# A gated-unit kernel: a small copy as the first DMA on the scalar queue, 512 bytes in each of sixteen rows

## Chip, cores and metric

One core of a Trainium2 chip. The metric is the device time of one execution in microseconds (us).

## The reference

```python
def setup_inputs():
    return {"x": np.random.randn(8192, 8192).astype(np.float32)}

def reference(x):
    a, b = np.split(x, 2, axis=-1)
    return a * (1 / (1 + np.exp(-b)))
```

268 MB are read, 134 MB written, and each output element costs one sigmoid and one multiply.

## The kernel before

The input is cut into 32 tiles of 256 rows. A tile puts two whole rows on each of 128 partitions, so one partition's part is a contiguous 64 KB of input and 32 KB of output. There are two input slots and two output slots in SBUF, the memory on the chip that the compute engines work from; DRAM holds input and output. Loads are issued on the sync queue, stores on the scalar queue. The first and the last tile are computed in four parts, the last is also stored in four parts.

```python
    R = 2
    SLOTS = 2
    n_tiles = n_rows // (P * R)
    x_t = x.rearrange("(n p r) m -> n p (r m)", p=P, r=R)
    out_t = out.rearrange("(n p r) m -> n p (r m)", p=P, r=R)
    ...
    for i in range(n_tiles):
        ...
        load = nc.sync.dma_start(out=xs[i % SLOTS], in_=x_t[i])
        ...
        def store(cols):
            ins = nc.scalar.dma_start(out=out_t[i, :, cols], in_=os[i % SLOTS][:, cols])
            now["stores"].append(ins)

        for k, (r, c) in enumerate(parts):
            b = rows[:, r, 1, c]
            sig = nc.scalar.activation(out=b, in_=b, func=SIG)
            mul = nc.vector.tensor_mul(out=packed[:, r, c], in0=rows[:, r, 0, c], in1=b)
            ...   # waits that others imply are removed by hand
            if i == n_tiles - 1 and k > 0:
                store(chunks[k - 1])
        store(chunks[-1] if i == n_tiles - 1 else slice(0, R * half))
```

## Time and profile before

| | before |
|---|---|
| median of five runs | 933.41 us (933.10 to 933.51) |
| span of the profiled run | 931.7 us |
| DVE (vector engine), ACT (scalar engine) busy | 278.7 us, 227.1 us |
| DMA rate over the span | 432 GB/s |

The queue rows: q1 is the sync queue (loads), q10 the scalar queue (stores).

```profile
q1 hardware_dynamic: 4608, 268.44, 66.6%
q10 hardware_dynamic: 5040, 134.22, 33.4%
```

The columns are packets, MB and share of the 16 engines' span: 4608 is 32 loads, each of 128 packets of 64 KB and 16 semaphore writes; 5040 is 31 stores of 128 packets of 32 KB, four of 128 packets of 8 KB, and 16 semaphore writes for each of the 35. And the timeline of the first 33 us on ACT, where store 0 is the first transfer on the scalar queue:

```profile
0.78 1.28 ACT L68 ACT_TABLE_LOAD   x1 [0.78 <-PEq L188]
21.95 7.31 ACT L68 ACTIVATE x_sb<-x_sb 128x2048 f32<-128x2048 f32 x4 [19.89 <-DMA x_sb<-in_x_dram]
32.82 0.38 ACTq L62 DMA_DIRECT2D out_dram<-o_sb  x1
```

The columns are start, duration, engine, line, operation, and in brackets the idle time before it and what ended it.

### The profile page before, as it was taken

Reading aid. Unit: us, or ns where it says so; the run is one execution under the profiler, and the core shown is the slowest. Engines: PE = TensorE matmul, PEld = TensorE weight load, DVE = VectorE, ACT = ScalarE, POOL = GpSimd, SP = SyncE. Lnnn points to the kernel's source line nnn. Section 1 sums busy time; section 2 is a strip of 40 time slices with the busy share of each in tenths; the row PEclk is TensorE's granted clock in tenths of the full one; section 3 lists DMA queues with packets and bytes.
Section 4 is the critical chain, followed back from the end, with each engine's and each line's share of the span. In section 5 each row is a group of like instructions: output and inputs, shape, how many; then the busy total and the mean of one; then the engine's idle time right before and its main releaser. Section 6 shows DMA issues by size and latency. Waiting matters only on the chain.

```text
span 931.7 us, 247 instructions
## 1 busy us (share of the span) xinstructions
DVE 278.7 (30%) x38; ACT 227.1 (24%) x39; POOL 0.2 (0%) x4
## 2 busy tenths in 40 slices
DVE  0333213333133331233312333123331233312333
ACT  1323330233311333113331133311333113332033
POOL 0000000000000000000000000000000000000000
DMA  9999999999999999999999999999999999999999
GB/s 405 428 450 428 422 456 405 450 428 428 450 418 438 428 436 442 428 428 450 447 408 428 442 459 428 413 460 411 450 428 425 453 408 447 428 428 450 425 430 405
DMA packets 9649, 402.67 MB, mean 432 GB/s; under 512 B 1072, under 2 KB 1072, under 8 KB 1072
## 3 DMA queue, kind: packets, MB, share of 16 engines
q1 hardware_dynamic: 4608, 268.44, 66.6%
q10 hardware_dynamic: 5040, 134.22, 33.4%
q14 instruction: 1, 0.01, 0.0%
HBM read 268.44 MB, written 134.22 MB: 432 GB/s over the span
## 4 chain that ended last, share of the span: by engine, by line
DMA 73%; DVE 15%; ACT 12%; issue 0%; ACTq 0%
DMA x_sb<-in_x_dram 73%; DVE o_sb L69 15%; ACT x_sb L68 12%; ACTq L62 0%; ACTq L68 0%
## 5 line engine op out<-in xcount | busy, mean ns | idle before, releaser
L69 DVE TENSOR_TENSOR o_sb<-x_sb 128x8192 f32<-128x8192 f32 (+1 forms) x38 | 278.7, 7344 | 647.1 <-ACT x_sb L68 647.1
L68 ACT ACTIVATE x_sb<-x_sb 128x8192 f32<-128x8192 f32 (+1 forms) x38 | 225.8, 5952 | 695.6 <-DMA x_sb<-in_x_dram 694.4
L68 ACT ACT_TABLE_LOAD x1 | 1.3, 1283 | 0.8 <-PEq L188 0.8
L188 POOL MEMSET const-bfloat16-1.0<- 128x1 bf16 x1 | 0.1, 102 | 0.0
L188 POOL MEMSET const-uint8-127<- 128x1 uint8 x1 | 0.1, 102 | 0.0
L188 POOL MEMSET const-float32-0.0<- 128x1 f32 x1 | 0.1, 99 | 0.2 <-issue 0.2
L188 POOL MEMSET const-float32-1.0<- 128x1 f32 x1 | 0.1, 99 | 0.0
## 6 DMA issues: line engine op xcount, KB each, us to landing
out_dram<-o_sb ACTq DMA_DIRECT2D x31, 4096.0 KB, 34.7
out_dram<-o_sb ACTq DMA_DIRECT2D x4, 1024.0 KB, 5.6
x_sb<-in_x_dram SPq DMA_DIRECT2D x32, 42.2
```

The costliest lines, as they stand in the source:

```text
L68: sig = nc.scalar.activation(out=b, in_=b, func=SIG)
L69: mul = nc.vector.tensor_mul(out=packed[:, r, c], in0=rows[:, r, 0, c], in1=b)
L188: nc = _bacc.Bacc("TRN2", target_bir_lowering=False, num_devices=1)
```

## The change

The likely intent is to pay a first-use cost of the scalar queue early. A copy of 512 bytes per row from DRAM to DRAM is issued there first. It writes wrong values into the corner of the output that store 0 overwrites later, so store 0 has to wait for it.

```diff
+    warm = nc.scalar.dma_start(out=out[0:16, 0:P], in_=x[0:16, 0:P])
+    tc.keep_in_program_order(warm)
+
     gone = [{k: [] for k in ("loads", "sigs", "muls", "stores")} for _ in range(SLOTS)]
```

## The prediction

> **What bounds the kernel now.** I read the page first, then the waits, then the stretches, then single packets in the trace. The head of the page and its DMA rows say that only transfers fill the span:
>
> ```profile
> span 931.7 us, 247 instructions
> DVE 278.7 (30%) x38; ACT 227.1 (24%) x39; POOL 0.2 (0%) x4
> DMA  9999999999999999999999999999999999999999
> HBM read 268.44 MB, written 134.22 MB: 432 GB/s over the span
> ```
>
> The reader is to see that no compute engine passes 30%, while the DMA row has a 9 in every slice. The chain of waits alternates a load of 42 us with 16 us of compute, which looks like a latency chain:
>
> ```profile
> 60.58 42.21 DMA x_sb<-in_x_dram
> 102.88 7.04 ACT x_sb L68
> 109.94 8.70 DVE o_sb L69
> 118.66 42.09 DMA x_sb<-in_x_dram
> ```
>
> It is not one. The load issued at 60.58 us lands at 102.79 us, but the load before it lands only at 73.6 us (the sigmoid of that tile starts at 73.65): two loads are always queued, and a load takes 42 us because it shares the engines with the other load and a store. The view of busy time by stretch confirms it: the rate is flat from the moment the stores begin.
>
> ```profile
> 33.00:61.00 28.00, 8.69 (x1) 7.03 (x1) 0.00 (x0) 1.00 1.03 431
> 90.00:870.00 780.00, 232.04 (x27) 189.84 (x27) 0.00 (x0) 1.00 1.00 434
> ```
>
> (The last three columns are PE clock, DMA share, GB/s.) The trace's packet records say it most sharply. I chained them, each packet to the one that starts where it ends, into 16 sequences, one per DMA engine. Each begins 1.00 to 2.05 us after the span's start, ends at 930.7 to 931.4 us, and has at most 0.3 us of gap in between. So **every nanosecond of engine time, per engine, is on the path that sets the end**. A 64 KB load packet takes 2.418 us, a 32 KB store packet 1.213 us, an 8 KB one 0.309 us, a semaphore write 0.009 us. Per engine: 256 x 2.418 + 248 x 1.213 + 32 x 0.309 + 67 x 0.009 = 930.3 us, minus about 2.2 us by which neighbouring records overlap (read from the chains), plus about 1.6 us of stalls, gives 929.7 us; observed from first start to last end: 928.7 to 930.2.
>
> **The stalls are what this change can touch.** Of 4096 load packets all but some 32 take 2.41 to 2.45 us. The first group of exceptions is in the opening packets of load 0: 15 of 16 take 2.64 to 3.37 us, 0.22 to 0.95 us too much. The second is one packet on each of the 16 engines that starts at 35.5 to 36.1 us, just before the first packet of store 0, the first transfer ever on the scalar queue: 3.09 to 3.49 us, on average 0.85 us too much. It can be seen in narrow stretches, because a packet is counted where its middle lies:
>
> ```profile
> 33.00:34.00 1.00, 0.00 (x0) 0.00 (x0) 0.00 (x0) 1.00 2.44 1049
> 35.00:36.00 1.00, 0.00 (x0) 0.00 (x0) 0.00 (x0) 1.00 3.06 983
> ```
>
> Stretch 33 to 34 holds 16 load packets (1049 GB/s for 1 us is 16 x 64 KB) and 2.44 us of mean busy time, so 2.44 us each. Stretch 35 to 36 holds 15 (983 GB/s) and 3.06 us, so 3.06 x 16 / 15 = 3.26 us each. At no later store is there such an excess: from 92.6 to 96.8 us the scalar queue is empty too, and store 2 starts without it. So the 0.85 us is a first-use cost, of the queue, of the output tensor, or of a store's direction; the trace of this kernel alone does not say which. Since the engines never idle, those 0.85 us are in the 933.41.
>
> **What the Trainium skill says.** Of the page "DMA: Bandwidth & Descriptors" I use three places. Its section "Bandwidth", under "Where 436 GB/s comes from", gives a ceiling of 435.2 GB/s for 16 engines; the trace's 434 GB/s in the long stretch agrees. 402.65 MB at 435.2 GB/s is 925.2 us (an estimate from the page's figure), so no change that keeps the bytes can gain more than about 8 us, 0.9%. Its section "Queues, rings and completion order" says that each engine round-robins between queue rows at packet granularity; the trace agrees, load and store packets alternate on every engine from 38.8 to 63.6 us. Its section "Why a DMA increments its semaphore by 16 and not by 1" says how many engines a transfer uses: the largest divisor up to 16 of the slowest dimension; sixteen rows give 16, so the copy touches every engine's scalar ring once. No run shows that yet. From "Perfetto Trace Analysis", section "DMA Instruction — HWDGE (DVE, Sync)", I take that the block which generates descriptors is locked for one issuer at a time.
>
> **The change part by part.** Nothing is removed. Built, the changed kernel has one more instruction on the scalar engine, ahead of the table load, and it shifts the rotation of eight DMA semaphores by one. After undoing that shift the orders and waits of all engines agree, but for two waits: store 0 waits also for the copy, and one early load (the fifth) waits for the copy's semaphore, which it reuses.
> - Issue on ACT: one, at 0.33 to 0.38 us (0.362 us median of the 35 store issues). The table load moves from 0.78 to about 1.14 us and ends at 2.42; the first sigmoid starts at 21.95 us, when load 0 lands. Slack 19.5 us: worth 0.
> - Load 1 is issued at 0.778 us, in the same moment as the copy. At worst it waits one issue, 0.36 us; its packets start only at 21.0 us. Worth 0.
> - Bytes: on each engine one packet of 512 bytes and one semaphore write. From 0.309 us for 8 KB and 2.418 us for 64 KB, a packet is 0.0077 us + 0.0368 ns per byte, so 512 bytes take 0.027 us; with 0.009 us for the semaphore, +0.04 us.
> - The two new waits: the copy should land within 10 us; store 0 is ready at 32.8 us and the fifth load at 89.4 us. Worth 0.
> - The first-use stall: -0.85 us if it now falls inside the stall that load 0 has anyway, 0 if it only moves from 35.5 us to the first packets of load 0, for the engines are full there as well.
>
> **The rivals.** (A) *The stall moves, the time stays*: 933.41 + 0.04 = 933.45. For it: in load 0 it took 1.0 us from the start of the issue to the first packet, so a copy issued at 0.78 arrives at about 1.8 us, while each engine already works on its first load packet. Store 0, issued at 32.82, did not stall the packet then in flight (+0.02 us) but the one after it, and was served after that one. The same order here puts the stall in the second load packet, 4.1 us on, beside nothing. (B) *The stall is hidden*: 933.41 - 0.85 + 0.04 = 932.60. For it: load 0's own stall lasts until about 2.1 us whatever the start of the packet (engines that start at 2.02 and 2.05 lose 0.22 and 0), so an arrival at 1.8 may overlap it. Only partly, then some 933.0. (C) *The stall belongs to the first transfer that reads SBUF, not to the queue*: the copy has a stall of its own and store 0 keeps its own: 933.41 + 0.85 + 0.04 = 934.3. For it: the copy reads DRAM, so it does not exercise that path; against it: ring and output tensor are what is new in both. (D) *A large loss by the new waits*: against it stand 22 us of slack and more. (E) *The phase between the queues shifts and load and store alternate worse*: against it, in 30 tiles the pattern repeats to 0.1 us and gaps are none.
>
> **Range and chances.** I give A 0.5, B or part of it 0.33, C 0.17: 0.5 x 933.45 + 0.33 x 932.7 + 0.17 x 934.3 = 933.35. I say 933.2, between A and B, as A and B together have 0.83. The three runs before spread over 0.13 us; for another session I allow about 0.4 us beyond the rivals' values: 932.2 to 934.6. Two per cent are 18.7 us, twice the whole distance to the ceiling, so faster by that has 0.01; slower needs a stall or a wait that nothing in the trace hints at, 0.01.
>
> **What would show each step right or wrong.** In the profile after: the scalar queue has 32 packets more (5072), 16 of them of 512 bytes; the table load starts some 0.35 us later; load 1 is issued by 1.2 us and store 0 within 1 us of 32.8 us; the stretch 35 to 36 us shows 2.42 us per load packet under A and B, over 3.2 under C. Under A the second load packets on the engines (4 to 7 us) take some 0.85 us more; under B they take 2.42 and load 0 lands no later than 21.9 us. Load 0's landing thus separates A (22.8) from B (21.9). The prediction is wrong if store 0 is issued late because of its new wait, if the copy occupies an engine for far more than 0.04 us, or if the long stretch falls below 434 GB/s.

## The result, and the profile after

The changed kernel takes 933.24 us (median of five, 933.09 to 933.64) against 933.41. The ratio is 0.9997, with a 95% interval of 0.9985 to 1.0009: the same. (A ratio here is the mean time of one kernel's fast runs over that of the other's of the same rounds, so not quite the ratio of the medians quoted.) The profiled run was the slowest of the five, 933.64, so its longer span says nothing.

The head of the page and its queue row, after:

```profile
span 932.3 us, 250 instructions
DMA  9999999999999999999999999999999999999999
q10 hardware_dynamic: 5072, 134.23, 33.4%
out_dram<-in_x_dram ACTq DMA_DIRECT2D x1, 8.0 KB, 9.0
```

The scalar queue has the 32 packets more that were expected, and the copy landed 9.0 us after its issue. The timeline of the same stretch of ACT:

```profile
0.79 0.62 ACTq L41 DMA_DIRECT2D out_dram<-in_x_dram  x1
1.44 1.28 ACT L71 ACT_TABLE_LOAD   x1 [1.44 <-PEq L191]
21.91 7.31 ACT L71 ACTIVATE x_sb<-x_sb 128x2048 f32<-128x2048 f32 x4 [19.19 <-DMA x_sb<-in_x_dram]
32.79 0.36 ACTq L65 DMA_DIRECT2D out_dram<-o_sb  x1
```

The copy's issue and the table load fit into the wait for load 0: the first sigmoid starts at 21.91 us where it started at 21.95, and store 0 is issued at 32.79 where it was at 32.82. The wait added to store 0 costs nothing. The view of busy time by stretch, after (last three columns: PE clock, DMA share, GB/s). It counts a packet in the stretch in which the packet starts, with its whole duration:

```profile
4.00:5.00 1.00, 0.00 (x0) 0.00 (x0) 0.00 (x0) 1.00 2.42 1049
35.00:36.00 1.00, 0.00 (x0) 0.00 (x0) 0.00 (x0) 1.00 3.08 918
90.00:870.00 780.00, 231.43 (x27) 189.79 (x27) 0.00 (x0) 1.00 1.00 434
```

Here is what decides between the rivals. "Stall" means here that a packet takes longer than packets of its size usually do. The stretch 4 to 5 us holds the second load packet of all 16 engines (1049 GB/s is 16 x 64 KB in 1 us), which take 2.42 us each: no stall before the copy. The stretch 35 to 36 us holds 14 load packets (918 GB/s) at 3.08 x 16 / 14 = 3.52 us each: the stall before store 0 is still there. It is neither hidden nor moved. In the packet records there is one 512-byte packet on each of the 16 engines; they take 0.027 us each, between 6.50 and 7.07 us, and the load packets around them take 2.418 to 2.420 us.

For the rest I sum, from the packet records, how much longer than usual (2.418, 1.213, 0.309 us) the data packets took, and divide by 16, so that the figure is us per engine: in the opening (0 to 3 us), from 3 to 30 us, and around store 0 (30 to 45 us).

| profile | opening | 3 to 30 us | around store 0 |
|---|---|---|---|
| before | 0.69 | 0.01 | 0.87 |
| after | 0.70 | 0.00 | 1.12 |

### The profile page after: what moved, and what is told of

Read it like the earlier page. It is cut to its first block, busy times and chain, and to the rows that moved or that the text cites. A ratio compares the mean times of both kernels' runs of the same rounds, so it can differ in the third digit from the quotient of the medians.

```text
span 932.3 us, 250 instructions
## 1 busy us (share of the span) xinstructions
DVE 278.6 (30%) x38; ACT 227.0 (24%) x39; POOL 0.2 (0%) x4
## 4 chain that ended last, share of the span: by engine, by line
DMA 73%; DVE 15%; ACT 12%; issue 0%; ACTq 0%
DMA x_sb<-in_x_dram 73%; DVE o_sb L72 15%; ACT x_sb L71 12%; ACTq L65 0%; ACTq L71 0%
```

## The experiments

The time could not tell the rivals apart: they differ by 0.8 us, and the interval is 1.1 us to either side. But the question has a sharp answer in single packets: what is the 0.9 us in front of store 0, if not the first use of the queue? Twelve further runs were made, one of them of the kernel before again; all gave the right output. The theories were named as they arose (their letters are not those of the rivals in the prediction):

- **S**: the first transfer that reads SBUF, of any size.
- **D**: the first write to an address region of the output.
- **L**: the arrival of the third load, issued together with store 0.
- **Q**: store packets that reach a scalar queue which has gone empty.
- **R**: the switch from a long run of loads alone to loads mixed with stores.
- **O**: once in an execution, with the first bulk read of SBUF by each engine.

### Does the stall scatter? (b1_before_again)

The kernel before, unchanged.

> The kernel before, unchanged, profiled once more, to see how far the stall before store 0 varies from run to run. So far: 0.85 us on average over the 16 engines without a small transfer (before), 1.10, 1.05 and 1.09 us in the three kernels with one. If the small transfer made it longer, this run shows 0.8 to 0.9 us; if that is scatter, it may show 1.0 or more.

Measured: 933.04 us; 0.89 us around store 0. Over all profiles in which the stall stays at the first whole store, the sums with something small first on the scalar queue are 1.12, 1.08, 1.10, 0.97 and 0.73, those of whole stores with nothing first 0.87, 0.89, 0.99, 0.92 and 0.93. The ranges overlap, so I do not claim that the copy lengthens the stall.

### A small transfer from SBUF (e1_sbuf_warm)

```diff
-    warm = nc.scalar.dma_start(out=out[0:16, 0:P], in_=x[0:16, 0:P])
+    seed = pool.tile([16, P], fp32, name="seed")
+    nc.gpsimd.memset(seed, 0.0)
+    warm = nc.scalar.dma_start(out=out[0:16, 0:P], in_=seed)
```

> The small transfer on the scalar queue reads a small SBUF tile (set to zero) in place of DRAM; destination and size as in the change. Theory S (the stall in the load packets before store 0 belongs to the first transfer that reads SBUF): no load packet over 2.45 us near 35.5 us. If the stall is then hidden in the opening stall of load 0, the time is about 0.8 to 1.1 us under before (932.3 to 932.6); if it only moves, load packets of 3.2 to 3.6 us at 4 to 7 us and the time of before within 0.3 us. Theory L (it belongs to the arrival of the third load, issued in the same moment as store 0, whatever the scalar queue does): load packets at 35.5 us stay at 3.1 to 3.6 us, time as before within 0.3 us. Theory D (it belongs to the first write to an address region of the output): stays as well.

Measured: 933.19 us, ratio 0.9997 (0.9983 to 1.0011). Around store 0: 1.08 us, and 15 packets (983 GB/s) take 3.25 x 16 / 15 = 3.47 us:

```profile
35.00:36.00 1.00, 0.00 (x0) 0.00 (x0) 0.00 (x0) 1.00 3.25 983
```

Theory S as stated falls: a read of 512 bytes per engine from SBUF does not take the stall away.

### Store 0 issued later (e2_store0_late)

```diff
+        if i == 0:
+            held = now
+        else:
+            if i == 1:
+                first = nc.scalar.dma_start(out=out_t[0], in_=os[0])
+                ...          # after the sigmoid of tile 1
```

> No small transfer; store 0 is issued only after the sigmoid of tile 1, at about 51.9 us, while the third load is issued at 32.8 us as before. Theories S and D: load packets of 35.5 us take 2.42 us and one load packet per engine between 54 and 58 us takes 3.1 to 3.6 us. Theory L: the long packets stay at 35.5 us and none is near 55 us.

Measured: store 0 was issued at 41.4 us, not 51.9, since load 1 lands earlier with no store beside it. The stretches of this run:

```profile
35.00:36.00 1.00, 0.00 (x0) 0.00 (x0) 0.00 (x0) 1.00 2.27 983
42.00:43.00 1.00, 0.00 (x0) 1.00 (x1) 0.00 (x0) 1.00 2.47 786
```

At 35 us, 15 packets take 2.27 x 16 / 15 = 2.42 us, though the third load was issued at 33.0 us, nearly as ever; at 42 us, 12 packets take 2.47 x 16 / 12 = 3.29 us, and the first store packets follow them. **Theory L falls; the stall goes with the first store.** The run, a single one, also took 952.3 us, 19 us more. The store queue then carries a backlog: the sigmoid of tile 5, at 163.56 us, waits for a store. Load packets in the rest of the run (45 to 920 us) lose 16.5 us per engine in many pieces of 0.1 to 0.8 us. Why those packets are slow there is not settled by these runs.

### Store 0 in quarters (e3_store0_parts, e8_quarters_together)

```diff
-            if i == n_tiles - 1 and k > 0:
+            if i in (0, n_tiles - 1) and k > 0:
...
-        store(chunks[-1] if i == n_tiles - 1 else slice(0, R * half))
+        store(chunks[-1] if i in (0, n_tiles - 1) else slice(0, R * half))
```

> No small transfer; store 0 goes out in four quarters, the first at about 26.2 us, the third load at 32.8 us as before. Theories S and D: the long load packets start at 28 to 29 us (or one packet slot away) and those at 35.5 us take 2.42 us. Theory L: they stay at 35.5 us.

Measured: 936.2 us. The packets are now 8 KB. There is no single long packet but several slightly long ones: 0.09 us up to 30 us and 0.47 us from 30 to 45 us, 0.56 us in all, beginning with the load packets that start at 28 us. So it begins with the first store again (against L), and it is smaller and spread. Its largest piece, 0.23 to 0.38 us on every engine, comes late, in the load packets that start at 39.3 to 39.9 us.

The second form kept all sigmoids and multiplies of tile 0 first and issued the four stores after them in the program:

```diff
+        if i == 0:
+            for c in chunks:
+                store(c)
+        else:
+            store(chunks[-1] if i == n_tiles - 1 else slice(0, R * half))
```

> No small transfer; store 0 goes out as four stores of 8 KB packets, issued one after the other at the time of store 0 (32.8 us and on). If the stall is the filling of a read-ahead that scales with the packet: no load packet near 35.5 us loses more than 0.3 us, and the sum over the next load packets stays under 0.7 us. If it is a fixed cost of the first bulk store: one load packet per engine loses 0.8 to 1.1 us as before.

Measured: 938.17 us, 0.03 and 0.32 us. It did not do what it was made for: the first store was still issued at 26.18 us, as its multiply ended, so it is the first form once more. Both lose time later for another reason: the multiply of tile 2 waits for store 0 until 90.4 us, the next load is late, and the engines run dry near 99 us.

### Touching all of store 0's destinations, and all partitions (e4_touch128, e11_seed128)

```diff
-    warm = nc.scalar.dma_start(out=out[0:16, 0:P], in_=x[0:16, 0:P])
+    warm = nc.scalar.dma_start(out=out_t[0, :, 0:P], in_=x_t[0, :, 0:P])
```

> The copy on the scalar queue from DRAM to DRAM now writes 512 bytes at the start of each of the 128 destinations of store 0's packets (8 per engine instead of 1). Theory D: the long load packets at 35.5 us shrink to 2.42 us. Theories S and L: they stay at 3.1 to 3.6 us. The copy itself should cost 8 x 0.03 = 0.24 us per engine in place of 0.04 us, so the time is 0.2 us over before under S and L.

Measured: 934.15 us, ratio 1.0004 (0.999 to 1.0018); around store 0 1.10 us. Each of the 128 destinations now had been written to before (the records do not name the engine that did it), and the stall is as before: 14 packets of 3.06 x 16 / 14 = 3.50 us.

```profile
35.00:36.00 1.00, 0.00 (x0) 0.00 (x0) 0.00 (x0) 1.00 3.06 918
```

The eight 512-byte packets should add 0.24 us, which the time neither shows nor excludes. The second form (its edit is shown against e1) reads them from SBUF:

```diff
-    seed = pool.tile([16, P], fp32, name="seed")
+    seed = pool.tile([P, P], fp32, name="seed")
     nc.gpsimd.memset(seed, 0.0)
-    warm = nc.scalar.dma_start(out=out[0:16, 0:P], in_=seed)
+    warm = nc.scalar.dma_start(out=out_t[0, :, 0:P], in_=seed)
```

> The small SBUF tile now has 128 partitions of 512 bytes, so that every partition is read and every destination of store 0 is written once before store 0, with packets of 512 bytes only (8 per engine). If the first touch of a partition or of an address were the cost: no stall at 35.5 us. Theories O and R: it stays at 0.85 to 1.1 us; 0.2 us over before.

Measured: 934.56 us in a single run; around store 0 0.73 us, at the low end but there on all 16 engines, each of which has a load packet 0.58 to 0.84 us too long.

```profile
35.00:36.00 1.00, 0.00 (x0) 0.00 (x0) 0.00 (x0) 1.00 2.18 721
```

(11 packets of 2.18 x 16 / 11 = 3.17 us.) **Theory D falls**, and so does a first touch of a partition.

### Letting the scalar queue go empty (e5_drain3)

```diff
+            if i in (8, 16, 24):
+                for s in last_stores[(i + 1) % SLOTS]:
+                    tc.add_manual_dep(ins.ins, s.ins.name, DEP, reason="the queue is empty first")
             now["stores"].append(ins)
```

This one mattered because before, the scalar queue never goes empty after store 0: store 1 is issued at 60.58 us, while packets of store 0 run until 63.6 us. My argument in the prediction that "store 2 starts without it" proved less than it seemed to.

> No small transfer; the stores of tiles 8, 16 and 24 are issued only when the store before them has landed, so that the scalar queue is empty before three full-size stores in the middle of the kernel. Theory Q (the stall comes whenever full-size store packets reach a scalar queue that has gone empty, as its read-ahead has to be filled again): load packets of 3.1 to 3.6 us just before the first packet of those three stores, 3 x 0.8 to 1.1 us, so a time 2.4 to 3.3 us over before. Theory O (it comes once in an execution, with the first bulk store): one stall at 35.5 us as before, none at the three stores, time within 0.5 us of before.

Store 8 was issued at 269.53 us, after store 7 had landed, and its first packets ran at 273.3 us. The stretches of this run:

```profile
35.00:36.00 1.00, 0.00 (x0) 0.00 (x0) 0.00 (x0) 1.00 2.95 918
270.00:271.00 1.00, 0.00 (x0) 0.00 (x0) 0.00 (x0) 1.00 0.91 393
271.00:272.00 1.00, 0.00 (x0) 0.00 (x0) 0.00 (x0) 1.00 1.51 655
```

At 35 us, 14 packets take 3.37 us; at 270 to 272 us, 6 and 10 load packets (393 and 655 GB/s) take 2.43 and 2.42 us, with the store packets right behind them. At stores 16 and 24 it is the same. **Theory Q falls.** The time, 937.04 us (ratio 1.0044, 1.0029 to 1.0059), is not within the 0.5 us that O said; the records put 2.05 us per engine into many small losses between 45 and 920 us, most of them after 769 us, not into the three stores. What makes them is open, as in e2.

### A copy of store size from DRAM (e7_copy32k)

```diff
-    warm = nc.scalar.dma_start(out=out[0:16, 0:P], in_=x[0:16, 0:P])
+    warm = nc.scalar.dma_start(out=out_t[0, 0:16, 0 : R * half], in_=x_t[0, 0:16, 0 : R * half])
```

> The copy from DRAM to DRAM on the scalar queue moves 32 KB per row instead of 512 bytes, one packet of store size per engine at about 6.5 us. Theory Q: a stall of 0.5 to 1.1 us in the load packet before it (4 to 7 us) and still one of 0.85 to 1.1 us at 35.5 us; the time is 1.2 us (the packet) plus 0.5 to 1.1 us over before. Theory O: a stall at 4 to 7 us and none at 35.5 us; 1.2 us over before. If neither: no stall at 4 to 7 us, the one at 35.5 us stays, 1.2 us over before; then bytes read from SBUF in bulk would be what matters.

Measured: 934.83 us, ratio 1.0014 (1.0001 to 1.0028), which is 1.3 us for a packet of 1.21 us. The stretches, at the load packets before the copy, at the copy and before store 0:

```profile
4.00:5.00 1.00, 0.00 (x0) 0.00 (x0) 0.00 (x0) 1.00 2.27 983
6.00:7.00 1.00, 0.00 (x0) 0.00 (x0) 0.00 (x0) 1.00 1.14 492
36.00:37.00 1.00, 0.00 (x0) 0.00 (x0) 0.00 (x0) 1.00 1.23 393
```

The load packets ahead of the copy take 2.42 us (15), the copies 1.22 us (15), the load packets before store 0 3.28 us (6 of them in this stretch). From 3 to 30 us only four load packets in all are long (together 0.24 us per engine), all of them after the copies, so most engines have none; around store 0 1.12 us remain. It is the third case named before the run: 32 KB written to DRAM through the scalar queue do not take the stall, so of what was proposed a bulk read of SBUF is left.

### A packet of store size from SBUF (e10_sbuf32k)

```diff
-    warm = nc.scalar.dma_start(out=out[0:16, 0:P], in_=x[0:16, 0:P])
+    nc.vector.memset(os[0][0:16, :], 0.0)
+    warm = nc.scalar.dma_start(out=out_t[0, 0:16, :], in_=os[0][0:16, :])
```

> The transfer on the scalar queue is now one packet of 32 KB per engine from SBUF (16 partitions of the first output tile, set to zero by VectorE first), at about 9 us. Theory O in the form 'once, with the first bulk read of SBUF by an engine': a stall of 0.8 us or more in a load packet before it and none at 35.5 us; time 1.2 us (the packet) over before. Theory R: little or no stall at 9 us, as only three load packets came before, and still one of 0.85 to 1.1 us at 35.5 us; 1.2 to 1.6 us over before.

The stretches of this run, two at the early packet and two before and at store 0, whose first packets come at 40.8 us here:

```profile
13.00:14.00 1.00, 0.00 (x0) 0.00 (x0) 0.00 (x0) 1.00 1.34 262
14.00:15.00 1.00, 0.00 (x0) 0.00 (x0) 0.00 (x0) 1.00 1.16 262
38.00:39.00 1.00, 0.00 (x0) 0.00 (x0) 0.00 (x0) 1.00 2.27 983
40.00:41.00 1.00, 0.00 (x0) 0.00 (x0) 0.00 (x0) 1.00 1.14 492
```

The early packets, 8 of 32 KB in each of the first two stretches (262 GB/s), take 1.34 x 16 / 8 = 2.68 us and 2.32 us in place of 1.213. The load packets ahead of store 0 take 2.42 us, and the first store packets (15 in the last stretch) 1.22 us: **no stall at store 0**, the only run of the fourteen profiled where that is so. In the sums: 1.40 us from 3 to 30 us, 0.00 around store 0. The time is 934.96 us, ratio 1.0016 (0.9999 to 1.0032), 1.5 us more: the packet's 1.21 us and some 0.3 us, as the loss was moved and not hidden. One thing weakens the size, not the finding: all 16 engines read at once from 16 neighbouring partitions, which may have slowed the early packets too; the 1.40 us need not all be the stall. (In the next run up to eight engines read such neighbouring partitions in the same moment, and no packet of 8 KB was slower for it; for 32 KB no run shows it.)

### The same with 8 KB (e12_sbuf8k)

The edit is shown against e10.

```diff
-    nc.vector.memset(os[0][0:16, :], 0.0)
-    warm = nc.scalar.dma_start(out=out_t[0, 0:16, :], in_=os[0][0:16, :])
+    nc.vector.memset(os[0][0:16, 0 : half // 2], 0.0)
+    warm = nc.scalar.dma_start(out=out_t[0, 0:16, 0 : half // 2], in_=os[0][0:16, 0 : half // 2])
```

> As the run that moved the stall (one packet per engine from the first output tile in SBUF), with 8 KB instead of 32 KB per engine. If any packet of some KB takes the whole stall: 0.8 to 1.3 us in or before the 8 KB packet, none at 35.5 us, time 0.3 us (the packet) over before. If the stall is paid in proportion to the first bytes: 0.2 to 0.4 us at the 8 KB packet and 0.5 to 0.8 us left at 35.5 us; time again 0.3 us over before. If the packet is too small to count, as 512 bytes were: 0.85 us or more still at 35.5 us; 0.3 us over before.

Measured: 934.45 us, ratio 1.0012 (0.9998 to 1.0025). The 8 KB packets take 0.309 us, nothing more (0.01 us from 3 to 30 us), and 0.97 us remain around store 0 (9 packets of 1.90 x 16 / 9 = 3.38 us in this stretch):

```profile
35.00:36.00 1.00, 0.00 (x0) 0.00 (x0) 0.00 (x0) 1.00 1.90 590
```

One packet of 8 KB per engine is too small to count, 32 KB is enough. Whether it is the size of one packet that counts, or the sum of the bytes read, these runs do not separate.

### Loads alone, then stores, in the middle (e9_loads_alone)

```diff
         now["loads"].append(load)
+        if i == 10:
+            for j in (8, 9):
+                late = nc.scalar.dma_start(out=out_t[j], in_=os[j % SLOTS])
+                tc.add_manual_dep(late.ins, load.ins.name, DEP, reason="a stretch of loads alone")
+                ...
         def store(cols):
+            if i in (8, 9):
+                return
```

> No small transfer; the stores of tiles 8 and 9 are held back until the load of tile 10 has landed, so that in the middle of the kernel each engine moves load packets alone for some 20 us, as it does before store 0, and then the stores come. The time will be several us over before, as later tiles wait for their output slots; only the packets count. Theory R (the stall is the switch from a long run of loads alone to loads mixed with stores, each time): a load packet of 3.1 to 3.6 us per engine just before the first packet of store 8, near 300 us. Theory O (once in an execution): none there, one at 35.5 us.

Measured: 939.55 us, the stores at 293.56 us. Some twelve load packets in a row ran on an engine before them. The stretches at store 0 and ahead of store 8:

```profile
35.00:36.00 1.00, 0.00 (x0) 0.00 (x0) 0.00 (x0) 1.00 3.11 983
295.00:296.00 1.00, 0.00 (x0) 1.00 (x1) 0.00 (x0) 1.00 2.29 918
```

At 35 us 15 packets take 3.32 us; at 295 us 14 take 2.62 us. In the records eight load packets lose up to 1.05 us there, so at least half of the engines lose nothing; it is 0.25 us per engine against 0.92 at store 0. So R is not the rule, but a smaller part of the same kind is not excluded. The stores' slots then come free late, the load queue runs dry near 332 us, and the first load packets after that take 1.4 us too long:

```profile
333.00:334.00 1.00, 0.00 (x0) 0.33 (x1) 0.00 (x0) 1.00 3.28 918
```

That is 14 packets of 3.75 us. In e3 and e8 the same happens at 100 us (1.42 and 1.38 us per engine). So the opening stall of load 0 seems to be of another kind than that of store 0: it came again in all three runs in which load packets started on engines that had run dry.

## Why the prediction was right, by its own steps

- **The number.** 933.2 was predicted, 933.24 measured. The sum that the runs support is 933.41 + 0.04 = 933.45, the number of rival A, but not by A's mechanism. That 933.2 came nearer is luck: it was a mean that gave weight to rival B, which did not happen, and 0.2 us are within the scatter of single runs.
- **DMA bound, no gain by engines.** Right: 434 GB/s in the long stretch before and after.
- **The copy's own cost, 0.04 us.** Right in the packet: 0.027 us for 512 bytes and 0.009 us for the semaphore, as worked out.
- **Issue on ACT, 0.36 us.** Off: 0.62 us, so the table load starts 0.66 us later. It costs nothing, as the slack is 19 us.
- **Load 1 and the two new waits.** Right: load 1 and store 0 are issued within 0.04 us of before. The fifth load is issued at 89.79 us in the same moment as store 2, as before (89.44), while the copy had landed by 9.8 us.
- **The packet order.** Right: the copy was served after the packet in flight and one more, at 6.5 us.
- **"-0.85 us if it now falls inside the stall that load 0 has anyway, 0 if it only moves".** This step failed. The stall did neither. It is no first use of the queue (the copy went through without one), nor of the output (e4, e11); what takes its place is a bulk read from SBUF (e10, one profile). The load packets before store 0 measured 3.52 us after the copy, where 2.42 us was expected under A and B. Rival C named that kind and had 0.17; it was wrong in giving the copy a stall of its own, and in "the first transfer that reads SBUF" of any size (e1, e12). What saved the number is that "stays" and "moves" cost the same on engines that are never idle.
- **The signs.** The stretch 35 to 36 us separated the rivals as it was meant to. Load 0's landing did not: the first sigmoid starts at 21.91 us, the value given for B, and B is false; a stall that stays at store 0 leaves load 0 alone as well.
- **A reading.** The prediction says that a stretch counts a packet where its middle lies. It counts it where it starts: the packets in 35 to 36 us start at 35.5 us and later, and last 3.3 us. Its sums per packet are not touched by this.

## What is shown and what is open

Shown: transfers in packets of 512 bytes do not remove the stall at store 0 (after, e1, e4, e11); the stall follows the first store (e2) and does not come back at three later stores that find the scalar queue empty (e5); 8 KB per engine from SBUF (e12) and 32 KB from DRAM (e7) do not take its place, 32 KB per engine from SBUF do (e10). The reading that fits all of these is that each DMA engine loses about 0.9 us once, when it first reads some 32 KB from SBUF. That one packet took the place of the stall rests on one kernel and one profile, and the 0.25 us per engine ahead of store 8 in e9 do not fit "once" well. Not shown: what inside the engine needs that time, and why 8 KB store packets (e3, e8) meet it in smaller pieces. No version beats both kernels clear of noise: the one that removes the stall from store 0 (0.9 us) adds a packet of 1.21 us per engine and has 1.40 us of lost time around it.

## What to carry to other kernels

Before adding a warm-up, ask whether the resource that it uses is ever idle: on engines that are full from 1 us on, as here, a first-use cost that is moved is still paid (e10), and the warm-up's own cost is added. A warm-up must resemble what it stands for in path and size; a 512-byte copy from DRAM prepared nothing for 32 KB stores from SBUF. And where the time's interval is wider than the effect, durations of single packets can still decide between theories.

## What the Trainium skill lacked or had wrong

- "DMA: Bandwidth & Descriptors": it has no one-off loss at an engine's first bulk read of SBUF. Thirteen of the fourteen profiles show one at the first store: 0.73 to 1.12 us per engine where it goes out whole, 0.3 to 0.5 us in pieces where it goes out in quarters. The fourteenth shows none there after one 32 KB packet from SBUF.
- The same page has first-byte latencies, but not that the first load packets on engines that ran dry themselves last longer; the excess is 0.6 to 0.7 us per engine at the start of all kernels here, and 1.36 to 1.42 us in the middle of three of them.
- The same page, section "SWDGE vs HWDGE vs iDMA", gives a packet, in its table on the software path, as preferably at most 4096 bytes, and has no figure in bytes for the hardware path that is used here. The records here have packets of 32 and 64 KB between which an engine switches queues. The copy's packet on each engine waited for two load packets, and its semaphore write (8.94 to 9.48 us) for one more: 8 KB took 9.0 us from issue to landing, where the section "Anatomy of one DMA — SWDGE (gpsimd) path" (another path) has about 2 us of fixed cost.
- "Perfetto Trace Analysis", section "DMA Instruction — HWDGE (DVE, Sync)", has the descriptor block locked for one issuer (it names the DVE and Sync sequencers as those that share it; here it is the scalar and the sync queue). The copy, issued 0.01 us after load 1, took 0.62 us, which fits; but before, store 0 and load 2, issued 0.004 us apart, took 0.38 and 0.33 us, which shows no wait of a whole issue. Source and destination in DRAM may be what made the copy's issue long; the runs do not separate the two.
